# HGRN scores of the short distances as 64x64 products in two column halves, three levels together

## The chip, the cores and the metric

The kernel runs on one core of a Trainium2 chip. The metric is device time in microseconds (us): before the change the median of three runs is 1633.6 us (1633.28 to 1634.9). The chip has a matrix engine (TensorE; PE in the profile, with its weight loads in a row of their own, PEld), a vector engine (VectorE, DVE), a scalar engine (ScalarE, ACT), GpSimd (POOL) and SyncE (SP), which issues the transfers from memory.

## The reference

One layer of a diffusion backbone over 256 latent tokens and 256 context tokens of width 2048: modulation vectors, an RMSNorm, one wide input projection, a convolution branch and a gated linear recurrence (HGRN) in two directions, a gated merge, an output projection and a squared-ReLU MLP. The change concerns the recurrence alone. For one head of width 128, one direction and one chunk of 64 tokens, the reference computes

```python
a = jnp.cumsum(gc, axis=2)
diff = a[:, :, :, None, :] - a[:, :, None, :, :]
decay = jnp.exp(jnp.where(tri[:, :, None], diff, -jnp.inf))
scores = jnp.einsum('bhtk,bhsk,bhtsk->bhts', qc, kc, decay)
intra = jnp.einsum('bhts,bhsv->bhtv', scores, vc)
s_new = jnp.exp(a_last[:, :, 0, :])[..., None] * s + \
    jnp.einsum('bhsk,bhsv->bhkv', kc * jnp.exp(a_last - a), vc)
```

so a score of token t for token s is a product over the 128 channels, in which each channel is damped by the forget gates between s and t. The state `s` carries what came before the chunk. There are eight heads, a forward and a backward scan, and four chunks of latent tokens.

## The kernel before, in words

Weights arrive as pages of 128x1024 f32 (`raw`), issued by SyncE. Each is split into a high part (`whi`, line 124, ScalarE) and a low part (`wlo`, line 127, VectorE), and TensorE forms three products a block (line 188, or lines 255 and 257 where two are joined). Four pages are held split ahead of use.

The recurrence runs beside these projections. It begins while the projections of the forget gates run (a loop over the eight heads, in which TensorE also forms the gates of the next head) and goes on under the two projections of the convolution branch, from about 215 to 480 us. Each head is a generator (`head`). The projections call `pump` every few products; `pump` gives up to three live generators a credit of about 1.95 us (1.1 to 1.3 in other places). A generator yields a cost, which is taken from the credit, or `None`, which ends its turn until the next pump. So the work of a head is strewn among the projections' products in the order of the program, and a scheduler then sets the final order on each engine.

`head` does not work chunk by chunk. It treats all 256 latent tokens of both directions at once by levels: level m holds the pairs of tokens that lie in the same block of 2m tokens, but in different halves of it. The tile `x6` holds, on 128 channels, keys and queries for both directions, already damped up to the current block size. The levels are m = 0 (a token with itself), 1, 2, 4, 8, 16, 32, 64 and 128. For each level

- ScalarE gathers the left operand into a contiguous tile (`left`, line 1454), where the two halves of each block come from different parts of `x6` (`halves`);
- TensorE forms two f32 products of 128x128 over 128 channels (line 1465), one for each block of 128 tokens, the right operand being read from `x6` in place by the same kind of gather;
- the result goes from the accumulator bank into the score tile `sc`: by a plain copy on ScalarE for m = 0 (line 1468) and m = 128 (line 1470), and by a copy under a mask on VectorE otherwise (`copy_predicated`, line 1472), since only some entries of the 128x128 block belong to the level;
- VectorE damps `x6` by one more level (lines 1480, 1481) and joins the gates (line 1483).

A level yields `None` between its left copy and its products, and 1.4 after the damping. After the last level come four transposes (line 1488), the context's state (line 1496), and the output, which reads `sc` (lines 1505 and 1507).

Small tiles of 128x256 f32 (`left`, `ksum`, `terms` and others) share six buffers, accumulators share eight banks, and the masks are loaded once, 128x896 numbers for seven levels.

One other stage matters for the prediction: the modulation vectors at the beginning (about 21 to 121 us) are products whose stationary operand has 32 columns. They are put on four strips of 32 columns of the array, by the partition at which the output begins:

```python
for j in range(4):
    g, n = 32 * j, 4 * t + j
    self.pe(nc.tensor.matmul, ps[g:g + 32, :], s32[:, 32 * n:32 * n + 32], w[:, j * T:(j + 1) * T], ...)
```

Of the kernel before, what the change touches and what calls it, by code (L numbers as in the profile page):

```python
# [8 lines left out]
F32 = mybir.dt.float32  # L9
F32R = mybir.dt.float32r  # L10
I32 = mybir.dt.int32
U8 = mybir.dt.uint8
# [3 lines left out]
P = 128  # L16
T = 256
D = 2048
# [8 lines left out]
TW = 1024  # L27
# [19 lines left out]
    _OFF[_n] = (_o, _w)  # L47
    _o += _w
NPACK = _o
LEVELS = (1, 2, 4, 8, 16, 32, 64)  # L50


class Stream:
# [84 lines left out]
class Kernel:  # L138
# [60 lines left out]

    def small(self, n, name):  # L200
        if n <= T:
            return self.sp.tile([P, T], F32, name=name, tag="t1", bufs=6)[:, :n]
        if n <= 512:
            return self.sp.tile([P, 512], F32, name=name, tag="t2", bufs=5)[:, :n]
        return self.page(F32, name)[:, :n]
# [180 lines left out]
    def run(self):  # L386
        nc, a = self.nc, self.a
        pack = self.cp.tile([P, NPACK], F32, name="pack")
# [21 lines left out]
        sc = self.cp.tile([P, 32], F32, name="silu_c")  # L410
# [119 lines left out]
        for i in range(2):  # L530
            ps = self.bank()
# [54 lines left out]
        def hx(i):  # L586
            return self.operand(hparts[i])
# [116 lines left out]
        for k in range(KT):  # L704
            ps = self.bank()[:, :T]
            nk = KT if k < WHOLE else KP
            for t in range(nk // 4):
                st.fetch_to(FETCH)
                w = st.whole()
                for j in range(4):  # L710
                    g, n = 32 * j, 4 * t + j
# [39 lines left out]
        for _ in forget:  # L751
            pass
        self.queued = None
        masks = self.cp.tile([P, 7 * P], U8, name="masks")
        mi = self.page(I32, "masks_in")[:, :7 * P]
        with self.tc.issue_after(st.dma.ins):
            nc.sync.dma_start(mi, a["masks"])
        self.load_row(0)
        nc.vector.tensor_copy(masks, mi)
        self.masks = masks.rearrange("p (l t) -> p l t", l=7)  # L760
        hlat = hx(0)
        for _ in self.values(1, hx, st.next, vb):
            pass
# [17 lines left out]
        for h in range(NH):  # L781
            accs = []
            for d in range(2 * (h > 0)):
                accs.append(self.bank())
                for hf in range(2):
                    hi, lo = st.next()
                    for k8 in range(8):
                        k = 8 * hf + k8
                        s = slice(k8 * P, (k8 + 1) * P)
# [629 lines left out]
    def head(self, h, e, vp):  # L1419

        nc = self.nc
        ev = e[:, :TW].rearrange("p (i t) -> p i t", t=T)
        for d in range(2):  # L1430
            s = e[:, 2 * d * T:2 * (d + 1) * T]
            nc.vector.tensor_scalar(out=s, in0=s, scalar1=self.lbm[:, 8 * d + h:8 * d + h + 1], scalar2=self.lb[:, 8 * d + h:8 * d + h + 1],
                                    op0=ALU.mult, op1=ALU.add)
        yield 0.7
        x6 = self.sp.tile([P, 6 * T], F32, name="x6", tag="x6", bufs=2)
        nc.scalar.activation(out=x6[:, 0:2 * T], in_=e[:, 0:2 * T], func=AF.Copy, scale=-1.0, bias=1.0)
        nc.scalar.activation(out=x6[:, 4 * T:6 * T], in_=e[:, 2 * T:4 * T], func=AF.Copy, scale=-1.0, bias=1.0)
        q = self.at(self.qp, h)
        nc.vector.tensor_tensor(x6[:, 2 * T:4 * T].rearrange("p (i t) -> p i t", t=T), ev[:, 2:0:-1, :],
                                q.rearrange("p (o t) -> p o t", o=1).broadcast_to([P, 2, T]), op=ALU.mult)  # L1440
        ks = self.small(T, "ksum")
        nc.vector.tensor_tensor(ks, x6[:, T:2 * T], x6[:, 4 * T:5 * T], op=ALU.add)
        yield 1.0
        sc = self.small(512, "sc")
        sc4 = sc.rearrange("p (c t) -> p c t", c=4)

        def halves(o, step, n, m):

            return bass.AP(x6.tensor, x6.offset + o, [x6.ap[0], [2 * m, n // (2 * m)], [step + m, 2], [1, m]])

        for n, m in enumerate((0, 1, 2, 4, 8, 16, 32, 64, 128)):
            if 0 < m < 128:
                left = self.small(T, "left")
                nc.scalar.copy(out=left.rearrange("p (n s m) -> p n s m", s=2, m=m), in_=halves(T, 3 * T, T, m))
            yield None
            ps = self.bank()
            for b in range(2):
                if m == 0:
                    w, r = ks[:, b * P:(b + 1) * P], q[:, b * P:(b + 1) * P]
                elif m < 128:  # L1460
                    w, r = left[:, b * P:(b + 1) * P], halves(2 * T + b * P, T, P, m)
                else:
                    w = x6[:, T:T + P] if b == 0 else x6[:, 4 * T + P:5 * T]
                    r = x6[:, 3 * T + P:4 * T] if b == 0 else x6[:, 2 * T:2 * T + P]
                nc.tensor.matmul(ps[:, b * P:(b + 1) * P], w, r, start=True, stop=True)  # L1465
            pv = ps[:, :T].rearrange("p (b t) -> p b t", b=2)
            if m == 0:
                nc.scalar.copy(out=sc4[:, 0::3, :], in_=pv)
            elif m == 128:
                nc.scalar.copy(out=sc4[:, 1:3, :], in_=pv)  # L1470
            else:
                nc.vector.copy_predicated(sc4[:, 0::3, :], self.masks[:, n - 1:n, :].broadcast_to([P, 2, P]), pv)
            if m == 0:
                continue
            lo = x6[:, 0:3 * T].rearrange("p (n w) -> p n w", w=2 * m)[:, :, 0:m]
            hi = x6[:, 3 * T:6 * T].rearrange("p (n w) -> p n w", w=2 * m)[:, :, m:2 * m]
            d = e[:, 0:4 * T].rearrange("p (n w) -> p n w", w=2 * m)
            nb = 3 * T // (2 * m)
            no = T // (2 * m)
            nc.vector.tensor_tensor(lo, lo, d[:, 0:nb, m:m + 1].broadcast_to([P, nb, m]), op=ALU.mult)  # L1480
            nc.vector.tensor_tensor(hi, hi, d[:, no:no + nb, 0:1].broadcast_to([P, nb, m]), op=ALU.mult)
            if m < 128:
                nc.vector.tensor_tensor(d[:, :, 0:1], d[:, :, 0:1], d[:, :, m:m + 1], op=ALU.mult)
            yield 1.4
        yield None
        pt = self.bank()
        for j, o in enumerate((0, P, 5 * T, 5 * T + P)):
            nc.tensor.transpose(out=pt[:, j * P:(j + 1) * P], in_=x6[:, o:o + P], identity=self.v["ident"])
        kt = self.small(512, "kt")
        nc.scalar.copy(out=kt, in_=pt)  # L1490
        yield None
        c = (h % 4) * P
        ps = self.bank()
        for d in range(2):
            for tb in range(2):
                nc.tensor.matmul(ps[:, d * P:(d + 1) * P], kt[:, (2 * d + tb) * P:(2 * d + tb + 1) * P],  # L1496
                                 vp[1][:, tb * 512 + c:tb * 512 + c + P], start=(tb == 0), stop=(tb == 1))
        st = self.small(T, "state")
        nc.scalar.copy(out=st, in_=ps[:, 0:T])
        yield None  # L1500
        po = self.bank()
        for tb in range(2):
            o = po[:, tb * P:(tb + 1) * P]
            for d in range(2):
                nc.tensor.matmul(o, x6[:, (3 - d) * T + tb * P:(3 - d) * T + (tb + 1) * P], st[:, d * P:(d + 1) * P], start=(d == 0), stop=False)  # L1505
            for sb in range(2):
                nc.tensor.matmul(o, sc[:, sb * T + tb * P:sb * T + (tb + 1) * P], vp[0][:, sb * 512 + c:sb * 512 + c + P], start=False, stop=(sb == 1))  # L1507
        if h % PB == 0:
            self.on.append(self.page(F32, "o"))
        o = self.at(self.on, h)  # L1510
        nc.scalar.copy(out=o, in_=po[:, :T])
        for tb in range(2):
            junk = self.small(P, "junk")
            nc.scalar.activation(out=junk, in_=o[:, tb * P:(tb + 1) * P], func=AF.Square, accum_out=self.osq[:, 2 * h + tb:2 * h + tb + 1])
        self.ended += 1
# [24 lines left out]
    def conv(self, uhv, uvv):  # L1540
# [70 lines left out]
            yield 1.2  # L1611


_IN = [("pack", (P, NPACK), F32), ("x", (T, D), F32), ("ctx", (T, D), F32), ("bgain", (4, TW), F32), ("gain", (4, TW), F32), ("masks", (P, 7 * P), I32),
       ("wms", (WHOLE * KT // 4, P, TW), F32), ("wm0", ((KT - WHOLE) * KP // 4, P, TW), F32), ("wmd", (KT - WHOLE, P, TW), F32), ("crow", (2, TW), F32), ("wmt", (64, P, TW), F32), ("wm1", (64, P, TW), F32), ("wi0", (16, P, TW), F32), ("wf0", (4, P, TW), F32), ("wi1", (80, P, TW), F32),
       ("wi2", (80, P, TW), F32),        ("wpw", (16, P, TW), F32), ("who", (16, P, TW), F32), ("wo", (32, P, TW), F32), ("w1", (128, P, TW), F32), ("w2", (128, P, TW), F32)]


def _masks():
    i = np.arange(P)  # L1620
    s, t = i[:, None], i[None, :]
    out = []
    for m in LEVELS:
        out.append((s // (2 * m) == t // (2 * m)) & (s // m != t // m))
    return np.concatenate([o.astype(np.int32) for o in out], axis=1)
# [68 lines left out]
```

## Time and profile before

| | |
|---|---|
| median of three runs | 1633.6 us |
| span of the profiled execution | 1632.6 us |
| TensorE busy | 1615.6 us (99%) |
| VectorE busy | 1162.2 us (71%) |
| ScalarE busy | 784.3 us (48%) |
| first and last start of the score products (line 1465) | 215.2 and 474.1 us |

The profile is taken from one execution; its span is the time from its first to its last instruction. The page lists the engines' busy times, the span in 40 slices, the chain of work that ended last, and the costliest groups of instructions. A group reads: line, engine, operation, output and inputs by name, shape, count, then busy time and mean duration in ns, then the idle time of the engine just before these instructions, and what ended it. A timeline row reads: start in us, duration in us, engine, line, operation, names, shape and count. An f32 product stands as two rows on TensorE, each with a weight load of its own.

### The profile page before, as it was taken

How to read it: one execution, taken by the hardware profiler on the slowest of the kernel's cores; microseconds unless marked ns; L12 is line 12 of the kernel's file. 1: busy time of each engine (PE TensorE's matmuls, PEld its weight loads, DVE VectorE, ACT ScalarE, POOL GpSimd, SP SyncE). 2: the span in 40 equal slices, each digit the busy share in tenths (PEclk: the TensorE clock that was granted, in tenths of full speed). 3: DMA queues.
4: the chain of work that ended last, by engine and by line, in shares of the span. 5: the costliest groups of instructions: out<-in, count | busy, mean ns of one | idle time of the engine just before them, and what ended most of it. 6: DMA issues, size and time to landing. Idle time of an engine off the chain costs nothing.

```text
span 1632.6 us, 21510 instructions
## 1 busy us (share of the span) xinstructions
PE 1615.6 (99%) x7939; PEld 1337.5 (82%) x7939; DVE 1162.2 (71%) x1686; ACT 784.3 (48%) x1094; POOL 52.0 (3%) x98
## 2 busy tenths in 40 slices
PE   7999999999999999999999999999999999999998
PEld 5668888888888888888888888888888888888887
DVE  5786887778868889977887676545665656665556
ACT  6553444434554444654446665444553455435543
POOL 0000000000000000000000001000110011001000
PEclk9999999999999999999999999999999999999999
DMA  9997954444566566787887478867887688677763
GB/s 377 402 379 281 324 175 151 149 152 135 194 202 219 182 192 205 236 279 267 320 302 254 142 259 256 287 197 235 289 283 227 217 255 284 231 240 241 232 217 114
DMA packets 109145, 391.22 MB, mean 240 GB/s; under 512 B 12912, under 2 KB 13680, under 8 KB 109040
## 3 DMA queue, kind: packets, MB, share of 16 engines
q1 hardware_dynamic: 102096, 368.60, 66.4%
q0 software_dynamic: 6656, 20.99, 4.3%
q8 instruction: 62, 1.02, 0.3%
q14 instruction: 43, 0.35, 0.1%
q10 hardware_dynamic: 288, 0.26, 0.0%
HBM read 379.32 MB, written 10.49 MB: 239 GB/s over the span
## 4 chain that ended last, share of the span: by engine, by line
PE 94%; DVE 2%; DMA 1%; issue 1%; ACT 1%; SPq 0%; ACTq 0%; DVEq 0%
PE bank L188 82%; PE bank L255 5%; PE bank L257 3%; PE bank L1465 2%; DVE wlo L127 1%; DMA x<-ctx 1%; ACT whi L124 0%; DMA raw<-who 0%; PE bank L1496 0%; PE bank L1507 0%; PE bank L1505 0%; DMA raw<-wpw 0%; DVE gacc L1301 0%; SPq L526 0%; PE bank L1360 0%
## 5 line engine op out<-in xcount | busy, mean ns | idle before, releaser
L127 DVE TENSOR_TENSOR wlo<-raw,whi 128x1024 fp32r<-128x1024 f32 x488 | 593.0, 1222 | 321.2 <-ACT whi L124 315.1
L124 ACT ACTIVATE whi<-raw 128x1024 fp32r<-128x1024 f32 x488 | 512.9, 1059 | 605.2 <-PE bank L188 388.5
L188 PE MATMUL bank<-whi,h 128*128 128x512 f32 x2160 | 674.1, 390 | 2.0 <-DVE h L673 1.2
L188 PEld LDWEIGHTS bank<-whi,h 128*128 128x128 f32 x2160 | 405.1, 188 | 88.0 <-DVE h L673 2.1
L188 PE MATMUL bank<-wlo,h 128*128 128x512 f32 x1080 | 420.7, 390 | 1.3 <-DVE wlo L127 1.3
L188 PEld LDWEIGHTS bank<-wlo,h 128*128 128x128 f32 x1080 | 202.8, 188 | 44.9 <-DVE wlo L127 3.5
L188 PE MATMUL bank<-whi,hidh 128*128 128x512 f32 x503 | 195.0, 388 | 0.0
L188 PE MATMUL bank<-wlo,hidh 128*128 128x512 f32 x503 | 195.0, 388 | 0.0
L188 PE MATMUL bank<-whi,hidl 128*128 128x512 f32 x503 | 195.0, 388 | 0.0
L188 PE MATMUL bank<-h,whi 128*128 128x512 f32 x512 | 166.2, 405 | 0.0
L188 PEld LDWEIGHTS bank<-whi,hidl 128*128 128x128 f32 x503 | 94.4, 188 | 19.5
L188 PEld LDWEIGHTS bank<-wlo,hidh 128*128 128x128 f32 x503 | 94.4, 188 | 19.3
L188 PEld LDWEIGHTS bank<-whi,hidh 128*128 128x128 f32 x503 | 94.4, 188 | 19.3
L188 PEld LDWEIGHTS bank<-h,whi 128*128 128x128 f32 x512 | 91.3, 189 | 20.6 <-issue 6.2
L188 PE MATMUL bank<-h,wlo 128*128 128x512 f32 x256 | 100.0, 391 | 0.0
L255 PE MATMUL bank<-h,whi 128*128 128x512 f32 x384 | 97.8, 396 | 0.0
L255 PEld LDWEIGHTS bank<-h,whi 128*128 128x128 f32 x384 | 69.0, 189 | 12.4
L1314 DVE SCALAR_TENSOR_TENSOR raw<-raw,silu_row 128x1024 f32<-128x1024 f32 x64 | 76.6, 1219 | 0.4 <-DMA raw<-wmt 0.3
L1301 DVE SCALAR_TENSOR_TENSOR gacc<-raw,silu_c,gacc 128x1024 f32<-128x1024 f32 x60 | 76.7, 1278 | 0.0
L188 PEld LDWEIGHTS bank<-h,wlo 128*128 128x128 f32 x256 | 48.1, 188 | 10.2
L257 PEld LDWEIGHTS bank<-h,wlo 128*128 128x128 f32 x384 | 52.4, 190 | 3.9
L257 PE MATMUL bank<-h,wlo 128*128 128x256 f32 x384 | 53.5, 282 | 0.0
(246 smaller groups left out, 1374.5 us busy)
## 6 DMA issues: line engine op xcount, KB each, us to landing
raw<-w SPq DMA_DIRECT2D x256, 512.0 KB, 4.8
raw<-wi SPq DMA_DIRECT2D x172, 512.0 KB, 4.5
raw<-wmt SPq DMA_DIRECT2D x64, 512.0 KB, 4.3
raw<-wm SPq DMA_DIRECT2D x64, 512.0 KB, 4.8
rawpage<-wm SPq DMA_DIRECT2D x42, 512.0 KB, 9.7
raw<-wo SPq DMA_DIRECT2D x32, 512.0 KB, 4.8
raw<-who SPq DMA_DIRECT2D x16, 512.0 KB, 5.1
raw<-wpw SPq DMA_DIRECT2D x16, 512.0 KB, 5.6
```

Source lines behind the costliest of these rows:

```text
L124: kn.his.append(nc.scalar.activation(out=hi, in_=raw, func=AF.Copy))
L127: kn.los.append(nc.vector.tensor_tensor(lo, raw, hi.bitcast(F32), op=ALU.subtract))
L188: ins = fn(*args, **kw)
L255: nc.tensor.matmul(bank, w[0][:, cut(i)], x(k)[2], start=(k == 0), stop=False)
L257: nc.tensor.matmul(bank[:, T:], w[1][:, cut(i)], x(k)[0], start=False, stop=(k == nk - 1))
L1301: nc.vector.scalar_tensor_tensor(acc, raw, s, acc, op0=ALU.mult, op1=ALU.add)
L1314: nc.vector.scalar_tensor_tensor(raw, raw, 1.0, self.srow, op0=ALU.mult, op1=ALU.mult, accum_out=self.dot[:, 32 * j + b:32 * j + b + 1])
L1465: nc.tensor.matmul(ps[:, b * P:(b + 1) * P], w, r, start=True, stop=True)
```

## The change

The levels from 0 to 64 lie within 128 tokens, and those up to 32 within 64. The change forms every level up to 64 as four products of 64x64: for each block of 128 tokens one for its first 64 tokens and one for its second 64. The results of the two go to the accumulator's partitions 0 to 63 and 64 to 127, and the products with them to the two column halves of the array. For m = 64 each half takes the other half's queries.

The nine levels are handled in three groups: (0, 1, 2), (4, 8, 16) and (32, 64, 128). Within a group the operands of all levels are prepared first, and the products follow together, into one bank, with m = 128 as before in a bank of its own. Since `x6` is damped between the levels of a group, the right operand must be kept too: for all levels but the last of a group it is copied on ScalarE (`right`), as the left one is. The masked copies now work on 128x128 numbers (`near2`), with masks for six levels of 64 columns. The near block is copied into its two places in `sc` at the end, by halves of the partitions, and so is the level m = 64, which needs no mask now. The small tiles have seven buffers in place of six.

```diff
-LEVELS = (1, 2, 4, 8, 16, 32, 64)
+LEVELS = (1, 2, 4, 8, 16, 32)
...
-            return self.sp.tile([P, T], F32, name=name, tag="t1", bufs=6)[:, :n]
+            return self.sp.tile([P, T], F32, name=name, tag="t1", bufs=7)[:, :n]
...
-        masks = self.cp.tile([P, 7 * P], U8, name="masks")
+        masks = self.cp.tile([P, 6 * 64], U8, name="masks")
...
+        near = sc[:, P:2 * P]
+        near2 = near.rearrange("p (b t) -> p b t", b=2)
...
-        for n, m in enumerate((0, 1, 2, 4, 8, 16, 32, 64, 128)):
-            if 0 < m < 128:
-                left = self.small(T, "left")
-                nc.scalar.copy(out=left.rearrange("p (n s m) -> p n s m", s=2, m=m), in_=halves(T, 3 * T, T, m))
-            yield None
-            ps = self.bank()
-            for b in range(2):
-                if m == 0:
-                    w, r = ks[:, b * P:(b + 1) * P], q[:, b * P:(b + 1) * P]
-                elif m < 128:
-                    w, r = left[:, b * P:(b + 1) * P], halves(2 * T + b * P, T, P, m)
-                else:
-                    w = x6[:, T:T + P] if b == 0 else x6[:, 4 * T + P:5 * T]
-                    r = x6[:, 3 * T + P:4 * T] if b == 0 else x6[:, 2 * T:2 * T + P]
-                nc.tensor.matmul(ps[:, b * P:(b + 1) * P], w, r, start=True, stop=True)
-            pv = ps[:, :T].rearrange("p (b t) -> p b t", b=2)
-            if m == 0:
-                nc.scalar.copy(out=sc4[:, 0::3, :], in_=pv)
-            elif m == 128:
-                nc.scalar.copy(out=sc4[:, 1:3, :], in_=pv)
-            else:
-                nc.vector.copy_predicated(sc4[:, 0::3, :], self.masks[:, n - 1:n, :].broadcast_to([P, 2, P]), pv)
-            if m == 0:
-                continue
+        def side(name, o, step, m):
+            t = self.small(T, name)
+            nc.scalar.copy(out=t.rearrange("p (n s m) -> p n s m", s=2, m=m), in_=halves(o, step, T, m))
+            return t
+
+        def decay(m):
             lo = x6[:, 0:3 * T].rearrange("p (n w) -> p n w", w=2 * m)[:, :, 0:m]
...
-            yield 1.4
+
+        for levels in ((0, 1, 2), (4, 8, 16), (32, 64, 128)):
+            ops = []
+            for m in levels:
+                if m == 0:
+                    ops.append((m, ks, q))
+                    continue
+                if m == 128:
+                    yield None
+                    break
+                left = side("left", T, 3 * T, m)
+                right = None
+                if m != levels[-1]:
+                    right = side("right", 2 * T, T, m)
+                ops.append((m, left, right))
+                yield None
+                if right is not None:
+                    decay(m)
+                    yield 1.2
+            ps = self.bank()
+            for n, (m, left, right) in enumerate(ops):
+                for b in range(2):
+                    for g in range(2):
+                        o = b * P + g * 64
+                        r = b * P + (1 - g) * 64 if m == 64 else o
+                        nc.tensor.matmul(ps[64 * g:64 * g + 64, n * P + b * 64:n * P + b * 64 + 64], left[:, o:o + 64],
+                                         right[:, r:r + 64] if right is not None else halves(2 * T + o, T, 64, m), start=True, stop=True)
+            if levels[-1] == 128:
+                far = self.bank()
...
+            for n, (m, _, _) in enumerate(ops):
+                pv = ps[:, n * P:(n + 1) * P].rearrange("p (b t) -> p b t", b=2)
+                if m == 0:
+                    nc.scalar.copy(out=near, in_=ps[:, n * P:(n + 1) * P])
+                elif m == 64:
+                    for g in range(2):
+                        nc.scalar.copy(out=sc4[64 * g:64 * g + 64, 0::3, 64 - 64 * g:128 - 64 * g], in_=pv[64 * g:64 * g + 64])
+                else:
+                    i = LEVELS.index(m)
+                    nc.vector.copy_predicated(near2, self.masks[:, i:i + 1, :].broadcast_to([P, 2, 64]), pv)
+            if levels[-1] == 128:
+                for g in range(2):
+                    nc.scalar.copy(out=sc4[64 * g:64 * g + 64, 0::3, 64 * g:64 * g + 64], in_=near2[64 * g:64 * g + 64])
+                nc.scalar.copy(out=sc4[:, 1:3, :], in_=far[:, :T].rearrange("p (b t) -> p b t", b=2))
+            decay(levels[-1])
+            yield 1.8
```

The order of the instructions moves with it. On TensorE, the first head's first two levels stood apart before, among the products of the gates' projection (`h` by `whi` and `wlo`, line 188):

```order
L1465 MATMUL bank<-q_1730,ksum 128x128 x2
L188 MATMUL bank<-h_685,whi 128x512 x2
L188 MATMUL bank<-h_685,wlo 128x512
L188 MATMUL bank<-h_750,whi 128x512 x2
L188 MATMUL bank<-h_750,wlo 128x512
L188 MATMUL bank<-h_819,whi 128x512 x2
L188 MATMUL bank<-h_819,wlo 128x512
L188 MATMUL bank<-h_882,whi 128x512 x2
L188 MATMUL bank<-h_882,wlo 128x512
L1465 MATMUL bank<-x_2161,left 128x128 x2
```

Now the first head's levels 0, 1 and 2 stand together (line 1495), twelve products of 64x64 in place of six of 128x128:

```order
L188 MATMUL bank<-h_882,whi 128x512 x2
L188 MATMUL bank<-h_882,wlo 128x512
L1495 MATMUL bank<-q_1730,ksum 64x64 x4
L1495 MATMUL bank<-right,left 64x64 x4
L1495 MATMUL bank<-x_2161,left 64x64 x4
L188 MATMUL bank<-h_955,whi 128x512 x2
L188 MATMUL bank<-h_955,wlo 128x512
```

The 64-column products form 27 unbroken stretches in the program, for 24 groups. Three groups are cut by projection rows ahead of their third level; here, still on TensorE, the first group of the sixth head, with the last group of the fifth behind it (line 1502 is m = 128):

```order
L1495 MATMUL bank<-q_1731,ksum 64x64 x4
L1495 MATMUL bank<-right,left 64x64 x4
L188 MATMUL bank<-h_370,whi 128x512 x2
L188 MATMUL bank<-h_370,wlo 128x512
L188 MATMUL bank<-h_458,whi 128x512 x2
L188 MATMUL bank<-h_458,wlo 128x512
L1495 MATMUL bank<-x_3436,left 64x64 x4
L188 MATMUL bank<-h_549,whi 128x512 x2
L188 MATMUL bank<-h_549,wlo 128x512
L188 MATMUL bank<-h_612,whi 128x512 x2
L188 MATMUL bank<-h_612,wlo 128x512
L1495 MATMUL bank<-right,left 64x64 x8
```

On ScalarE, the copies of the first head stand between the high parts of the weights (line 124); before, one left copy a level, here with the semaphores each waits for:

```order
L1468 COPY sc<-bank 128x2x128 [waits PE_49]
L124 ACTIVATE whi<-raw 128x1024 [waits DMAHW4_49,PE_49]
L1454 COPY left<-x_2161 128x256 [waits DVE_49] x2
L124 ACTIVATE whi<-raw 128x1024 [waits DMAHW5_49,PE_49]
L630 ACTIVATE fg<-bank 128x512 [waits PE_49]
L1454 COPY left<-x_2161 128x256 [waits DVE_49]
```

and now left and right copies (line 1456) and the near block's copy (line 1506) in the same place:

```order
L1456 COPY left<-x_2161 128x256 [waits DVE_49]
L124 ACTIVATE whi<-raw 128x1024 [waits DMAHW4_49,PE_49]
L1506 COPY sc<-bank 128x128 [waits PE_49]
L1456 COPY left<-x_2161 128x256 [waits DVE_49]
L1456 COPY right<-x_2161 128x256
L1456 COPY left<-x_2161 128x256 [waits DVE_49,Activation_49]
L1456 COPY right<-x_2161 128x256
L124 ACTIVATE whi<-raw 128x1024 [waits DMAHW5_49,PE_49]
```

There are 56 left copies as before, 40 right copies that are new, and the copies of a group stand one to four between two high parts. Eight of the 96 wait for TensorE, which none of the 56 did.

More of the change, by code (lines that the diff above doesn't have):

```diff
@@ L753, in run @@
         self.queued = None
-        masks = self.cp.tile([P, 7 * P], U8, name="masks")
-        mi = self.page(I32, "masks_in")[:, :7 * P]
+        masks = self.cp.tile([P, 6 * 64], U8, name="masks")
+        mi = self.page(I32, "masks_in")[:, :6 * 64]
         with self.tc.issue_after(st.dma.ins):
@@ L759, in run @@
         nc.vector.tensor_copy(masks, mi)
-        self.masks = masks.rearrange("p (l t) -> p l t", l=7)
+        self.masks = masks.rearrange("p (l t) -> p l t", l=6)
         hlat = hx(0)
@@ L1483, in head @@
                 nc.vector.tensor_tensor(d[:, :, 0:1], d[:, :, 0:1], d[:, :, m:m + 1], op=ALU.mult)
-            yield 1.4
+        for levels in ((0, 1, 2), (4, 8, 16), (32, 64, 128)):
[26 more added lines that the diff above has]
+                far = self.bank()
+                for b in range(2):
+                    w = x6[:, T:T + P] if b == 0 else x6[:, 4 * T + P:5 * T]
+                    r = x6[:, 3 * T + P:4 * T] if b == 0 else x6[:, 2 * T:2 * T + P]
+                    nc.tensor.matmul(far[:, b * P:(b + 1) * P], w, r, start=True, stop=True)
+            for n, (m, _, _) in enumerate(ops):
[14 more added lines that the diff above has]
+            yield 1.8
@@ L1611, in conv @@
             yield 1.2
-_IN = [("pack", (P, NPACK), F32), ("x", (T, D), F32), ("ctx", (T, D), F32), ("bgain", (4, TW), F32), ("gain", (4, TW), F32), ("masks", (P, 7 * P), I32),
+_IN = [("pack", (P, NPACK), F32), ("x", (T, D), F32), ("ctx", (T, D), F32), ("bgain", (4, TW), F32), ("gain", (4, TW), F32), ("masks", (P, 6 * 64), I32),
        ("wms", (WHOLE * KT // 4, P, TW), F32), ("wm0", ((KT - WHOLE) * KP // 4, P, TW), F32), ("wmd", (KT - WHOLE, P, TW), F32), ("crow", (2, TW), F32), ("wmt", (64, P, TW), F32), ("wm1", (64, P, TW), F32), ("wi0", (16, P, TW), F32), ("wf0", (4, P, TW), F32), ("wi1", (80, P, TW), F32),
@@ L1619, in _masks @@
 def _masks():
-    i = np.arange(P)
-    s, t = i[:, None], i[None, :]
+    s, t = np.arange(P)[:, None] % 64, np.arange(64)[None, :]
     out = []
```

## The prediction

> **What bounds the kernel now.** I read the page first: the engines' shares, the slices, the granted clock and the chain that ended last.
>
> ```profile
> span 1632.6 us, 21510 instructions
> PE 1615.6 (99%) x7939; PEld 1337.5 (82%) x7939; DVE 1162.2 (71%) x1686; ACT 784.3 (48%) x1094; POOL 52.0 (3%) x98
> PE   7999999999999999999999999999999999999998
> PEclk9999999999999999999999999999999999999999
> PE 94%; DVE 2%; DMA 1%; issue 1%; ACT 1%; SPq 0%; ACTq 0%; DVEq 0%
> PE bank L188 82%; PE bank L255 5%; PE bank L257 3%; PE bank L1465 2%; DVE wlo L127 1%; DMA x<-ctx 1%; ACT whi L124 0%; DMA raw<-who 0%; PE bank L1496 0%; PE bank L1507 0%; PE bank L1505 0%; DMA raw<-wpw 0%; DVE gacc L1301 0%; SPq L526 0%; PE bank L1360 0%
> ```
>
> TensorE is busy in every slice at the full granted clock, and 94% of the chain is its work. The score products (line 1465) hold 2% of the chain: about 33 us. A change of the scores is therefore worth what it takes off or adds to TensorE's stream of rows; the other engines count only where they make that stream wait. Next come the busy times of the stretch in which the heads run, and the groups of that stretch (window 212 to 480 us).
>
> ```profile
> core 0: us, PE busy (x) PEld busy (x) DVE busy (x) ACT busy (x) POOL busy (x), PEclk, DMA share, GB/s
> 215.00:480.00 265.00, 264.33 (x1469) 228.69 (x1468) 209.04 (x394) 113.11 (x215) 1.45 (x2) 1.00 0.49 159
> ```
>
> ```profile
> L1465 PE MATMUL bank<-x,left 128*128 128x128 f32 x224 | 36.2, 287 | 0.7 <-ACT left L1454 0.5
> L1465 PEld LDWEIGHTS bank<-x,left 128*128 128x128 f32 x224 | 31.6, 191 | 4.4 <-ACT left L1454 2.9
> L1472 DVE COPY_PREDICATED sc<-masks,bank 128x256 f32<-128x256 uint8 x56 | 24.9, 445 | 34.0 <-PE bank L1465 33.7
> L1454 ACT COPY left<-x 128x256 f32<-128x256 f32 x56 | 23.5, 427 | 50.1 <-DVE x L1481 49.9 <-DVE x L1439 0.2
> L1465 PE MATMUL bank<-q,ksum 128*128 128x128 f32 x32 | 4.9, 275 | 0.0
> L1514 ACT ACTIVATE junk<-o 128x128 f32<-128x128 f32 x14 | 4.2, 303 | 0.1
> ```
>
> In these 265 us TensorE is idle for 0.7 us, VectorE for 56 and ScalarE for 152. Each f32 product stands as two weight loads and two matmul rows (seven middle levels x 8 heads x 2 products make the 224 rows). Busy times overlap, so they are no prices; starts in the timeline are.
>
> **What the change removes.** One ordinary level on TensorE:
>
> ```profile
> 224.96 0.39 PE L188 MATMUL bank<-h,wlo 128*128 128x512 f32 x1
> 225.19 0.60 PE L1465 MATMUL bank<-x,left 128*128 128x128 f32 x4
> 225.55 0.71 PE L188 MATMUL bank<-h,whi 128*128 128x512 f32 x2
> 226.10 0.39 PE L188 MATMUL bank<-h,wlo 128*128 128x512 f32 x1
> 226.33 0.61 PE L188 MATMUL bank<-h,whi 128*128 128x512 f32 x2
> 226.78 0.39 PE L188 MATMUL bank<-h,wlo 128*128 128x512 f32 x1
> ```
>
> From 226.10 to 226.78 stand three steps of the projection: 0.68 us, 0.227 a step. From 224.96 to 226.10 stand three steps and the level: 1.14 us. A level costs 0.46 us. Its four rows start 0.11 us apart (0.60 less the last row's own 0.275, over three). Nine levels x 8 heads = 72, so 33.1 us. The level of distance 1 costs more:
>
> ```profile
> 218.34 0.39 PE L188 MATMUL bank<-h,wlo 128*128 128x512 f32 x1
> 218.57 0.82 PE L1465 MATMUL bank<-x,left 128*128 128x128 f32 x4
> 219.09 0.77 PE L188 MATMUL bank<-h,whi 128*128 128x512 f32 x2
> 219.70 0.39 PE L188 MATMUL bank<-h,wlo 128*128 128x512 f32 x1
> ```
>
> 1.36 us instead of 1.14 for the same rows: 0.22 more, x 8 heads = 1.8 us. I put it down to the moving operand, which is gathered element by element there; the change copies it first, so this goes. Waits for the left copy cost between 0.7 us (TensorE's own idle, above) and 2.9 (its weight loads'); I take 1.5. Removed in all: 33.1 + 1.8 + 1.5 = **36.4 us**.
>
> **What it adds on TensorE.** Eight levels per head become 4 products of 64x64, 8 rows: 8 x 8 x 8 = 512 rows. If the two column halves run side by side these are 256 pairs. Rows on parts of the array's columns are in this trace: the modulation stage runs on four 32-column strips.
>
> ```profile
> L188 PE MATMUL bank<-rawpage,s 128*32 128x256 f32 x400 | 25.5, 383 | 0.0
> L188 PEld LDWEIGHTS bank<-rawpage,s 128*32 128x32 f32 x400 | 11.4, 109 | 11.4 <-issue 5.1 <-ACT v L1416 0.4
> ```
>
> ```profile
> 88.89 1.07 PE L188 MATMUL bank<-whi,h 128*128 128x512 f32 x4
> 89.89 1.50 PE L188 MATMUL bank<-rawpage,s 128*32 128x256 f32 x24
> 91.32 0.72 PE L188 MATMUL bank<-h,whi 128*128 128x512 f32 x2
> 91.89 0.40 PE L188 MATMUL bank<-h,wlo 128*128 128x512 f32 x1
> ```
>
> 24 rows of 256 moving elements fit between 89.89 and 91.32: 0.060 us a row. One alone would take twice the 0.11 of a 128-element row, 0.22; so four strips overlap fully, and six sets of 0.22 explain 1.32 of the 1.43 us. They also stand one strip after the other in the program, as the halves of the change do. A 64x64 row has half the moving elements and half the weight columns of today's 128x128 row: 0.055 us. The weight loads say the same: 191 ns for 128 columns, 109 for 32, so 0.85 ns a column and 0.055 us of streaming for 64. I take 0.055 a pair: 256 x 0.055 = **14.1 us**. The lower end is 0.05 (12.8); the upper is 0.055 a row, 0.11 a pair, as if nothing overlapped (28.2).
>
> The product of distance 128 stays as it is: 8 x 0.46 = **3.7 us**.
>
> New is the change of array shape. From 88.89 to 91.89 pass 3.00 us; the four and two 128x512 steps in it account for 1.36, the six sets for 1.32. What is left, 0.32 us, is one excursion into column strips and back. The weight loads show where:
>
> ```profile
> 89.89 1.02 PEld L188 LDWEIGHTS bank<-rawpage,s 128*32 128x32 f32 x24 [0.35 <-issue]
> 91.32 0.30 PEld L188 LDWEIGHTS bank<-h,whi 128*128 128x128 f32 x2 [0.41 <-issue]
> ```
>
> ```profile
> PEld bank L188 <- issue: 12.0, 32, 0.4
> ```
>
> No semaphore ends these idles; 32 of them are the ways in and out of 16 such stretches. In the order of the changed program there are 27 stretches of 64-column products (three groups x 8 heads, three of them cut in two by projection rows): 27 x 0.32 = **8.6 us**. The lower end is half of that, 4.3, if narrower sets drain sooner; the upper 0.41 each, 11.1.
>
> [...]
>
> **Waits.** A group needs up to five copies where a level needed one. ScalarE makes five right copies more per head (0.427 each), one near-block copy instead of a wider one, and four quadrant copies of at most the 0.3 of a 128x128 one: some 3.3 us a head, 26 in all. Its 152 idle us cover them; it is then busy for 139 of 265. What is queued behind them on ScalarE is the high part of the next weights, and TensorE's projection waits for that. The chain before a group is shorter than before a level in one respect: the decay no longer waits for the previous level's product. That wait was
>
> ```profile
> DVE sc L1472 <- PE bank L1465: 33.7, 23, 4.1
> DVE x L1480 <- PE bank L1465: 2.1, 1, 2.1
> PEld bank L1465 <- ACT left L1454: 2.9, 8, 0.7
> ```
>
> Against that, eight of the copies now also wait for TensorE, since their buffer still holds operands of an earlier group. Waits cost between nothing and 27 times the 0.36 us of today's late copies (2.9 over 8), 9.8. I take **2.9**, as often late as now: the last copy of a group is still made one pump, some 12 projection steps, ahead.
>
> **Off the path.** VectorE's masked copies go from 56 of 128x256 to 48 of half the size, at most 12 of its 24.9 us saved; it has 56 idle, so nothing comes of that. The masks' load and cast shrink to 3/7 at about 212 us, where the DMA share is 0.49 and TensorE waits for neither: nothing. The old score copies on ScalarE are counted in the 3.3.
>
> **Sum.** Added: 14.1 + 3.7 + 8.6 + 2.9 = 29.3 us; removed 36.4; net 7.1 us less. The profiled span of 1632.6 goes to 1625.5. The median of the runs, 1633.6, is 1.0 above the span; I keep that: **1626.5 us**.
>
> **Rivals.**
> *Rows set the pace, not the halves.* Slower. Place: inside the 64-column stretches. If each row pair (weight load and matmul) needs 0.055 us whatever half it is on, the 512 rows take 28.2 us, not 14.1. The net is +7.0: 1640.6. It decides from 0.083 us a pair on (0.055 + 7.1/256), where the gain is zero. For it: the trace shows no train of rows faster than 0.060 us each, so nothing proves that more than one per 0.055 can be started. Against it: that train was held by its 256 moving elements, and four rows of a set overlap. Chance 0.16.
> [...]
> *The waits come back.* Every group stops for its third copy as today's late levels do: 27 x 0.36 = 9.8 instead of 2.9, net -0.2, so 1633.4. For it: ScalarE waits 49.9 us for VectorE ahead of its left copies, and the planner itself cut three groups in two, ahead of the third operand. Against it: only eight of 72 levels are late now. Chance 0.12.
> *The excursions are nearly free.* At 0.10 us, 5.9 less: 1620.6. [...] Against it: both idles are there in all 16 stretches. Chance 0.07.
>
> **How the numbers follow.** The forecast has 0.65, with its own range 1622.5 to 1631 from the ends of pair pace, excursion and waits partly together. A measurement of this kernel tells about 0.2% from no change (3.3 us: below 1630.3 faster, above 1636.9 slower). Faster: 0.62 of the forecast and the free excursions, 0.69. Same: 0.03 and the waits, 0.15. Slower: the row pace, 0.16. The range for 8 in 10 reaches from the free excursions past the waits and leaves out the row pace and a little below: 1620.5 to 1636.
>
> **What would show it.** The rows of line 1495 in pairs, about 7 ns and then 0.05 us apart, would bear out the overlap; evenly spaced at 0.05 or more, the first rival. A stretch of 24 rows should take 0.66 us from first to last start, and about 0.32 more around it, with "issue" idles at 54 weight loads. L1465's waits on the left copy should stand in the same few us under line 1495. It is wrong if a pair takes over 0.083 us, if excursions cost over 0.58 (8.6 + 7.1 over 27), or if TensorE's idle in the stretch grows by several us.

## The result

The changed kernel takes 1624.24 us (median of five runs, 1623.7 to 1626.58) against 1633.6 us before: 0.9946 of the time, 95% interval 0.9936 to 0.9956. Run again beside the experiments it took 1624.62 us against 1633.02, ratio 0.9947 (0.9934 to 0.9959). It is faster by 8.4 to 9.4 us; forecast were 7.1, with 1626.5 us as the time.

The page of the changed kernel, the lines that answer to those of before:

```profile
span 1621.9 us, 22046 instructions
...
PE 1606.9 (99%) x8195; PEld 1322.7 (82%) x8195; DVE 1154.8 (71%) x1678; ACT 804.7 (50%) x1166; POOL 52.2 (3%) x98
...
PEclk9999999999999999999999999999999999999999
...
PE 92%; DMA 5%; DVE 1%; issue 1%; ACT 1%; SPq 0%; ACTq 0%; DVEq 0%
```

TensorE is still the bound, at the full granted clock, with 256 rows more than before and 8.7 us less busy time. The chain now puts 5% down to transfers, where it was 1%; all but one of those stretches lie before 117 us, ahead of the heads, and TensorE stays 99% busy. The two profiled spans differ by 10.7 us, but not all of that is the change. The projection of line 255 stands on both sides of the heads (before the change its rows run from 168.0 to 211.5 us and again from 411.7 to 515.3), so its first and last start bracket the stage. The first line is of the kernel before, the second of the change:

```profile
L255 PE MATMUL bank<-h,whi x384: 387/393/534, 168.0 to 515.3; 128*128 128x512 f32 x192
```

```profile
L255 PE MATMUL bank<-h,whi x384: 387/393/500, 166.3 to 505.5; 128*128 128x512 f32 x192
```

Between these marks pass 347.3 us before and 339.2 now: **8.1 us less**. The first mark comes 1.7 us earlier in the profile of the change. Of this, 1.5 us stands already where the load of the masks is issued (123.5 us against 125.0), ahead of the recurrence; over all profiles here the mark lies between 166.3 and 168.5 us. Another 0.9 us is gained behind the last mark. I count neither. The same stretch measures every experiment below.

One group of the change, its levels 4, 8 and 16 for the first head, in TensorE's timeline, and its weight loads:

```profile
225.50 0.39 PE L188 MATMUL bank<-h,wlo 128*128 128x512 f32 x1
225.82 0.69 PE L1495 MATMUL bank<-right,left 128*64 128x64 f32 x16
226.34 0.40 PE L1495 MATMUL bank<-x,left 128*64 128x64 f32 x8
226.67 0.73 PE L188 MATMUL bank<-h,whi 128*128 128x512 f32 x2
227.24 0.40 PE L188 MATMUL bank<-h,wlo 128*128 128x512 f32 x1
```

```profile
225.82 0.55 PEld L1495 LDWEIGHTS bank<-right,left 128*64 128x64 f32 x16 [0.35 <-issue]
```

24 rows lie between 225.82 and 226.67. From 225.50 to 227.24 pass 1.74 us; less three projection steps of 0.227 the group costs 1.06 us, where three levels cost 3 x 0.46 = 1.38 before. The idle of 0.35 us on the way in is the one that the column strips showed. It is idle time of the weight loads, and a projection row still runs beside most of it: the first score row starts 0.32 us after that row (225.50 to 225.82) instead of 0.227, so 0.09 us of it delays TensorE's rows.

The busy times of the window 215 to 480 us, and its groups of instructions (these from 205 us on):

```profile
215.00:480.00 265.00, 265.00 (x1782) 222.64 (x1781) 203.81 (x388) 139.63 (x297) 1.46 (x2) 1.00 0.49 163
```

```profile
L1495 PE MATMUL bank<-right,left 128*64 128x64 f32 x320 | 14.2, 227 | 0.0
...
L1456 ACT COPY left<-x 128x256 f32<-128x256 f32 x56 | 23.7, 424 | 36.6 <-DVE x L1467 32.4 <-DVE x L1439 3.8 <-PE bank L1495 0.3
L1456 ACT COPY right<-x 128x256 f32<-128x256 f32 x40 | 17.0, 426 | 0.0
...
L1512 DVE COPY_PREDICATED sc<-masks,bank 128x128 f32<-128x128 uint8 x48 | 14.3, 297 | 4.0 <-PE bank L1495 3.8
```

ScalarE went from 113 to 139.6 us, as worked out (139). The profile shows no idle time of TensorE. VectorE's masked copies wait 3.8 us for score products where they waited 33.7; whether VectorE's relief is worth anything is tested below, by giving it work back.

### The profile page after: what moved, and what is told of

Its sections match the earlier page's. It is cut to its first block, busy times and chain, and to the rows that moved or that the text cites. A ratio compares the mean times of both kernels' runs of the same rounds, so it can differ in the third digit from the quotient of the medians.

```text
span 1621.9 us, 22046 instructions
## 1 busy us (share of the span) xinstructions
PE 1606.9 (99%) x8195; PEld 1322.7 (82%) x8195; DVE 1154.8 (71%) x1678; ACT 804.7 (50%) x1166; POOL 52.2 (3%) x98
## 3 DMA queue, kind: packets, MB, share of 16 engines
q8 instruction: 64, 1.05, 0.3%
## 4 chain that ended last, share of the span: by engine, by line
PE 92%; DMA 5%; DVE 1%; issue 1%; ACT 1%; SPq 0%; ACTq 0%; DVEq 0%
PE bank L188 80%; PE bank L255 5%; PE bank L257 3%; DMA raw<-wi 2%; DMA rawpage<-wm 1%; PE bank L1495 1%; DMA rawpage<-wms 1%; DMA x<-ctx 1%; PE bank L1541 0%; PE bank L1539 0%; PE bank L1530 0%; DVE wlo L127 0%; DMA raw<-wpw 0%; PE bank L1502 0%; ACT whi L124 0%
## 5 line engine op out<-in xcount | busy, mean ns | idle before, releaser
L255 PEld LDWEIGHTS bank<-h,whi 128*128 128x128 f32 x384 | 69.0, 189 | 12.6
```

Source lines behind the costliest of these rows:

```text
L255: nc.tensor.matmul(bank, w[0][:, cut(i)], x(k)[2], start=(k == 0), stop=False)
```

## The experiments

Times are medians; "stage" is the stretch between the first and last start of line 255, read from one profile each, and the table's last column is its difference to 347.3 us. The text often compares with the change, 339.2 us. Each ratio is to the kernel before as it was run on the same chip: 1633.6 us for the change, 1633.2 for the next four rows, 1633.0 for the last four.

| kernel | time | ratio to before (95%) | stage | against before |
|---|---|---|---|---|
| before | 1633.6, 1633.2, 1633.0 | 1 | 347.3 | |
| the change | 1624.24 | 0.9946 (0.9936 to 0.9956) | 339.2 | -8.1 |
| groups, full width | 1630.64 | 0.9986 (0.9978 to 0.9995) | 345.4 | -1.9 |
| halves in turn | 1634.92 | 1.0011 (1.0001 to 1.0020) | 349.5 | +2.2 |
| no groups | 1639.26 | 1.0038 (1.0025 to 1.0052) | 353.8 | +6.5 |
| two groups | 1620.83 | 0.9926 (0.9913 to 0.9938) | 335.0 | -12.3 |
| before, right copy at 1 | 1632.18 | 0.9995 (0.9986 to 1.0004) | 346.0 | -1.3 |
| strips of 32 | 1618.04 | 0.9909 (0.9896 to 0.9923) | 331.8 | -15.5 |
| masked copies twice | 1625.39 | 0.9951 (0.9938 to 0.9963) | 339.1 | -8.2 |
| the change again | 1624.62 | 0.9947 (0.9934 to 0.9959) | 339.2 | -8.1 |

The stage differences and the medians' agree within 1.3 us.

### Groups at full width

The edit is shown against the change, with the products' new arguments shortened to "...":

```diff
-                for b in range(2):
-                    for g in range(2):
-                        ... 64x64 products of block b, half g, into ps[64 * g:64 * g + 64, ...]
+                for b in range(2):
+                    nc.tensor.matmul(outs[n][:, b * P:(b + 1) * P], left[:, b * P:(b + 1) * P],
+                                     right[:, b * P:(b + 1) * P] if right is not None else halves(2 * T + b * P, T, P, m), ...)
...
-LEVELS = (1, 2, 4, 8, 16, 32)
+LEVELS = (1, 2, 4, 8, 16, 32, 64)
```

The masks have 128 columns and seven levels again, and the results go to `sc` in place, as before the change.

> The three groups, the right copies and the moments of the masked copies as in the change, but every level as two 128x128 products and masks of 128 columns as before: grouping without the column halves. Theory (the halves' overlap is most of the gain, less what the excursions cost): rows as before, 72 levels x 0.44 us = 31.7, plus 24 ends of 0.02, against 36.4 to 37 before: about 4.5 us faster than before, 1629. Rival (grouping and the copied right operand are the gain, by fewer waits): as fast as the change, 1624. Rival (the smaller masked copies on VectorE are the gain): no faster than before, 1633.6.

1630.64 us: 2.6 us of the 9 are had by grouping and copying. The first rival (as fast as the change) is out; the second (no faster than before) is out by little, since the interval of the ratio ends at 0.9995. The theory asked for 4.5 us and got 2.6 (1.9 in the stage). The timeline gives a reason; here the second and third level of a group:

```profile
363.99 0.61 PE L1491 MATMUL bank<-right,left 128*128 128x128 f32 x4
365.64 0.75 PE L1491 MATMUL bank<-x,left 128*128 128x128 f32 x4 [1.05 <-ACT left L1454]
```

```profile
PEld bank L1491 <- ACT left L1454: 2.1, 3, 1.2
```

The weight loads of three groups wait 2.1 us in all for a late left copy, and TensorE itself is idle for 1.4 us of that (1.05 in the group shown). Grouping alone does not do away with these waits.

### The halves in turn

```diff
-            for n, (m, left, right) in enumerate(ops):
-                for b in range(2):
-                    for g in range(2):
+            for g in range(2):
+                for n, (m, left, right) in enumerate(ops):
+                    for b in range(2):
```

> The change with one edit in the order of the products of a group: all products of the first column half, then all of the second, instead of by turns. The same 27 stretches and the same work. Theory (the halves overlap because neighbours in the program are on different halves): nothing overlaps, 512 rows x 0.058 us = 29.7 instead of 14.9, so 14.8 us slower than the change, about 1639, and a stretch of 24 rows takes 1.4 us. Rival (each half has a queue deep enough to run ahead): as the change, 1624, stretch 0.70 us.

1634.92 us: slower than the change by 10.3 us in the stage, and slower than before. The products are the same; only their order in a group differs. A stretch of 24 rows:

```profile
226.40 0.68 PE L1495 MATMUL bank<-right,left 128*64 128x64 f32 x8
226.91 0.22 PE L1495 MATMUL bank<-x,left 128*64 128x64 f32 x1
226.92 0.27 PE L1495 MATMUL bank<-right,left 128*64 128x64 f32 x1
...
227.44 0.40 PE L1495 MATMUL bank<-x,left 128*64 128x64 f32 x4
227.76 0.73 PE L188 MATMUL bank<-h,whi 128*128 128x512 f32 x2
```

The first half's 12 rows are eight with a right copy and four with a gathered right operand (x); then the second half's come in the same order. From the first row to the next projection row 1.36 us pass, where the change takes 0.85. The rows of one half start 0.058 us apart, no faster than the pairs of the change. The second half's first row starts at 226.92, beside the ninth of the first half: the other half runs ahead over three or four rows, and no farther. So the overlap comes from neighbours in the program on different halves.

The miss (10.3 us for 14.8) is this short overlap at the seam. The group above loses 1.36 - 0.85 = 0.51 us, while 12 rows one behind the other instead of beside would be 12 x 0.058 = 0.70: about 0.19 us is saved at its seam. Each of the 24 groups has one seam; the three that are cut in two have theirs in the second part, since the first part holds rows of one half alone. 14.8 - 24 x 0.19 = 10.2, and 10.3 were measured. The trace agrees: from the first row of a stretch to the next row behind it, the 27 stretches take 29.35 us in all, and 19.03 in the change.

### No groups

```diff
-        for levels in ((0, 1, 2), (4, 8, 16), (32, 64, 128)):
+        for levels in ((0,), (1,), (2,), (4,), (8,), (16,), (32,), (64, 128)):
...
```

Level 0 alone is followed by no damping, and the yield behind a group is 1.4, as before the change.

> 64x64 products in two column halves as in the change, but a group for each level alone (64 and 128 stay together), so 64 stretches in place of 27; no right copies but at 64. Theory (each excursion costs about 0.34 us of TensorE): 37 x 0.34 = 12.6 us slower than the change, and the gather of distance 1 up to 1.8 back: 1637 to 1639, slower than before. Rival (excursions are hidden or free, the halves alone are the gain): 1624 to 1626.

1639.26 us: 14.6 us more than the change in the stage (12.6 to 14.4 expected). The column halves without the grouping are slower than the kernel before. One level alone, then a level of distance 1, then a level with a late copy:

```profile
328.80 0.39 PE L188 MATMUL bank<-h,wlo 128*128 128x512 f32 x1
329.12 0.45 PE L1496 MATMUL bank<-x,left 128*64 128x64 f32 x8
329.50 0.73 PE L188 MATMUL bank<-h,whi 128*128 128x512 f32 x2
330.06 0.40 PE L188 MATMUL bank<-h,wlo 128*128 128x512 f32 x1
...
219.35 0.55 PE L1496 MATMUL bank<-x,left 128*64 128x64 f32 x8
...
456.21 0.45 PE L1496 MATMUL bank<-x,left 128*64 128x64 f32 x8 [0.49 <-ACT left L1456]
```

From 328.80 to 330.06 pass 1.26 us; less three steps of 0.227 that leaves 0.58 us for four pairs of rows, against 0.46 for the level at full width.

Not all of the 14.6 us is excursions. The right operand of distance 1 is gathered again here, and its eight levels take 0.10 us more each (0.55 for 0.45), 0.8 in all; one late copy holds TensorE for 0.5. The 37 further stretches are left with 13.3 us, 0.36 each.

### Two groups

```diff
-        for levels in ((0, 1, 2), (4, 8, 16), (32, 64, 128)):
+        for levels in ((0, 1, 2, 4), (8, 16, 32, 64, 128)):
...
-            return self.sp.tile([P, T], F32, name=name, tag="t1", bufs=7)[:, :n]
+            return self.sp.tile([P, T], F32, name=name, tag="t1", bufs=10)[:, :n]
...
-NPAGE = 30
+NPAGE = 29
```

> The change with two groups, (0, 1, 2, 4) and (8, 16, 32, 64, 128), in place of three; ten small buffers in place of seven, for which one of 30 pages is given up. 16 stretches in place of 27. Theory: 11 x 0.34 = 3.7 us faster than the change, 1620.5. Rival (longer groups make TensorE wait for ScalarE's copies, or the lost page delays the weights): not faster than the change, 1624 to 1628.

1620.83 us, 4.2 us better than the change in the stage (3.7 expected). A stretch of 32 rows:

```profile
218.90 0.39 PE L188 MATMUL bank<-h,wlo 128*128 128x512 f32 x1
219.22 0.45 PE L1495 MATMUL bank<-q,ksum 128*64 128x64 f32 x8
219.50 0.64 PE L1495 MATMUL bank<-right,left 128*64 128x64 f32 x16
219.97 0.41 PE L1495 MATMUL bank<-x,left 128*64 128x64 f32 x8
220.30 0.73 PE L188 MATMUL bank<-h,whi 128*128 128x512 f32 x2
220.87 0.39 PE L188 MATMUL bank<-h,wlo 128*128 128x512 f32 x1
```

From 218.90 to 220.87: 1.97 less 0.68, so 1.29 us for 16 pairs. With the 1.06 us that 12 pairs took in the change this gives both prices of the change, and the 0.58 for 4 pairs checks them: (1.29 - 1.06) / 4 = **0.058 us a pair**, and 1.06 - 12 x 0.058 = **0.36 us an excursion** (0.35 from the level alone).

### The right copy at distance 1, in the kernel before

```diff
+            if m == 1:
+                right = self.small(T, "right")
+                nc.scalar.copy(out=right.rearrange("p (n s m) -> p n s m", s=2, m=m), in_=halves(2 * T, T, T, m))
...
-                    w, r = left[:, b * P:(b + 1) * P], halves(2 * T + b * P, T, P, m)
+                    w, r = left[:, b * P:(b + 1) * P], halves(2 * T + b * P, T, P, m) if m > 1 else right[:, b * P:(b + 1) * P]
```

> The kernel before with one edit: at distance 1 the right operand is copied first too, as the change does, so the products read it in one piece (seven small buffers). Theory (the 0.22 us that a level of distance 1 costs beyond the others is the gathered moving operand): 8 x 0.22 = 1.8 us faster than before, about 1631.5, and the four rows of that level start 0.11 us apart. Rival (it has another cause, such as the weight loads of the gathered tile): as before, 1633.3.

The time can't be told from before (0.9995, 0.9986 to 1.0004). The rows can:

```profile
217.34 0.39 PE L188 MATMUL bank<-h,wlo 128*128 128x512 f32 x1
217.57 0.60 PE L1468 MATMUL bank<-right,left 128*128 128x128 f32 x4
217.93 0.71 PE L188 MATMUL bank<-h,whi 128*128 128x512 f32 x2
218.48 0.39 PE L188 MATMUL bank<-h,wlo 128*128 128x512 f32 x1
```

From 217.34 to 218.48 pass 1.14 us, as with an ordinary level, not 1.36: the gathered moving operand was the cause. The stage is 1.3 us shorter, where 1.8 were expected.

### Strips of 32

On top of the two groups, the levels 0, 1, 2 and 4:

```diff
+                for n, (m, left, right) in enumerate(ops):
+                    for b in range(2):
+                        for g in range(4):
+                            o = b * P + g * 32
+                            nc.tensor.matmul(ps[32 * g:32 * g + 32, n * 64 + b * 32:n * 64 + b * 32 + 32], left[:, o:o + 32],
+                                             right[:, o:o + 32] if right is not None else halves(2 * T + o, T, 32, m), start=True, stop=True)
```

Their block is then copied into the near block by quarters of the partitions, and the masks of the levels 1, 2 and 4 are laid out for 32 columns.

> The two groups of the last experiment, with the levels 0, 1, 2, 4 as 32x32 products in four column strips (64 rows a group where there were 32), and four more small copies on ScalarE a head. Theory (each part of the array keeps its own pace, which goes with its columns and moving elements): a set of four rows takes about 0.03 us, 16 sets 0.48 us instead of 0.93, 8 x 0.45 = 3.6 us faster than the two groups, 1617. Rival (a row with its weight load cannot start oftener than every 0.029 us, and the pairs of the change stand at that bound): 64 rows take 1.86 us, 7.4 us slower than the two groups, 1628.

1618.04 us, 3.2 us better than two groups in the stage, and the fastest kernel here: 0.9909 of before. 64 rows in one stretch:

```profile
249.90 0.33 PE L1497 MATMUL bank<-q,ksum 128*32 128x32 f32 x16
250.05 0.45 PE L1497 MATMUL bank<-right,left 128*32 128x32 f32 x30
...
250.59 0.73 PE L188 MATMUL bank<-h,whi 128*128 128x512 f32 x2
```

From 249.90 to 250.59 lie 64 rows, 16 on each of the four strips and each with a weight load: 0.011 us a row. The rival, a bound of 0.029 us on a row's start, is out.

### Masked copies twice

```diff
                     nc.vector.copy_predicated(near2, self.masks[:, i:i + 1, :].broadcast_to([P, 2, 64]), pv)
+                    nc.vector.copy_predicated(near2, self.masks[:, i:i + 1, :].broadcast_to([P, 2, 64]), pv)
```

> The change with every masked copy on VectorE issued twice, which leaves the result the same and gives VectorE 48 x 0.30 = 14 us more, as much as the change took off it and some more. Theory (VectorE's time is off the path): within 1 us of the change, 1624 to 1625. Rival (the waits that the change lost, about 2 us, went because VectorE has less to do): 2 us or more slower than the change, 1626 to 1628.

1625.39 us, and the stage as long as with the change (339.1 to 339.2). Busy times of the stage:

```profile
215.00:480.00 265.00, 265.00 (x1780) 222.59 (x1779) 213.62 (x438) 139.38 (x298) 1.46 (x2) 1.00 0.49 163
```

The second copies take 48 x 0.299 = 14.3 us. VectorE is busy 9.8 us more in this window, and TensorE still shows no idle time. VectorE's relief by the change is no part of its gain.

### The change again

> The change itself, beside the others on the same chip: 1624, 9 to 10 us faster than before, as first measured.

1624.62 us, 8.4 us faster than before; its stage is 339.2 us, as first.

## Why the prediction was right, step by step

**The bound.** Right: TensorE's stream counted. Giving VectorE 48 masked copies back moved nothing, though the groups at full width show that a late copy of ScalarE does hold TensorE (1.05 us in the group shown).

**What is removed (36.4 us).** It fits, but no run measures it alone. Added work by the measured prices below is 28.2 us (14.8, 9.7 and 3.7); with the 8.1 gained the removed part would be 36.3. That the level of distance 1 cost more because of its gathered right operand, which was only argued, is shown by the right copy in the kernel before.

**Pairs (14.1 us at 0.055).** Right in kind, 5% low: 256 x 0.058 = 14.8. The trace has the sign that was named: in the group shown, the two rows of a pair start 0.006 to 0.007 us apart, and the next pair 0.051 to 0.052 after them (0.10 behind the first pair). The halves overlap, as the four strips let expect; the halves in turn show what they cost when most of them don't (10.3 us).

**Excursions (27 x 0.32 = 8.6).** 27 x 0.36 = 9.7. The price taken from 32-column strips fits 64 columns and was a little low. The number of stretches, read from the order, foretold two kernels: 37 more cost 13.3 us and 11 fewer saved 4.2, 0.36 and 0.38 each. The lower end, half the price, was an estimate: no run shows that narrower sets drain sooner, nor a drain by itself; what was measured is 0.32 us an excursion with 32 columns (the modulation stage before) and 0.36 with 64. Without grouping, 64 of them turn the gain into a loss (6.5 us more than before).

The sign that the prediction named for them did not come, though. It expected idle time at 54 weight loads, on the ways in and out; the trace of the change shows 17 such idles of 0.35 to 0.37 us, all on the way in (listed under the waits, below). The other ten stretches follow rows of 128 or 256 elements, and the idle there is 0.12 to 0.13. Behind a group, where the strips had 0.41, the next projection's weight load shows none marked: it starts 0.07 us after the end of the group's last (226.28 + 0.32 = 226.60):

```profile
226.28 0.32 PEld L1495 LDWEIGHTS bank<-x,left 128*64 128x64 f32 x8
226.67 0.30 PEld L188 LDWEIGHTS bank<-h,whi 128*128 128x128 f32 x2
```

So the idle is no measure of the price; starts of rows are. In the group shown above 0.09 us of the 0.36 passes before the first row, 0.12 between the next two projection steps (226.67 to 227.24, 0.57 where two steps take 0.45), and the rest within and right behind the stretch. Nor are all 32 idles that the prediction counts ways in and out of strips: one, at 955 us, lies far from any.

**The product of distance 128 (3.7).** Unchanged.

**Waits (2.9 us).** Too high; it is the largest error of the sum, and the one that made the forecast too small. In the trace of the change:

```profile
PEld bank L1495 <- issue: 3.5, 10, 0.4
PEld bank L1495 <- ACT left L1456: 1.1, 3, 0.4
PEld bank L1495 <- PE bank L188: 1.1, 3, 0.4
PEld bank L1495 <- ACT fg L630: 0.4, 1, 0.4
```

The three that are put down to the left copy are 0.37 us each, hardly longer than the 0.35 of those with no releaser: I take them for the same idle on the way in, and see no copy that is late by more than 0.02 us. Why the late copies are gone is open. Grouping alone is not the reason, since the full-width groups have 2.1 us of them; VectorE's time is not either, since doubling its masked copies brings none back. Two groups show none among their waits (2.5 us in seven idles with no releaser, 0.4 in one put down to `x`), though they hold eight more right copies. The order of the instructions differs in each, and I did not separate it.

**Off the path.** Right in effect. The masks are loaded at 125 us and cast at 133 us, not at about 212; their cast on VectorE goes from 0.62 to 0.35 us, ahead of the stage.

**The rivals.** *Rows set the pace* is refuted twice, by 0.029 us a row in the change and 0.011 in the strips of 32. But the halves in turn lose most of the overlap, as that rival would (1634.9 us; it put the change at 1640.6): the danger was real and had another place, the order of the products. *The waits come back* did not happen (see the waits). *The excursions are nearly free* is refuted by no groups.

**The sum.** 36.4 removed less 28.2 added is 8.2 us; the stage got 8.1 us shorter, and 7.1 were forecast. That the forecast came so near is in part luck: waits of 2.9 us that did not come were set off by pairs and excursions taken 1.8 us too low. What the median has beyond the stage, 0.3 to 1.3 us, is not explained by the change.

## What to carry to other kernels

In this kernel, small f32 products gained from column parts of the array only when neighbours in the program stood on different parts, and when enough of them stood together to pay for the way in and out: here 0.36 us of TensorE, so a stretch must save more than that (a single level saved 0.23 in rows, 0.46 less 4 x 0.058, and lost). Count the stretches in the final order, not the loops: each one more or fewer was worth 0.36 to 0.38 us. Longer groups, and then narrower parts, each added to the gain (1624.6, 1620.8, 1618.0 us).

## What the runs showed of the hardware

Four strips of 32 columns together took 64 rows with their weight loads in 0.69 us; I had thought the start of a row might bind, at 0.055 us in a rival of the prediction and at 0.029 in a later one; 0.011 us a row were measured. A half that was free started its products past the other half's, but only over three or four rows: with one half's 12 rows ahead of the other's a group took 1.36 us to the next projection row, with the halves by turns 0.85. An f32 moving operand gathered in single elements made a level of four rows of 128 elements 0.22 us longer (1.36 us against 1.14 with its three projection steps), and with the operand copied first it took 1.14.
